# A two-layer hybrid attention transformer on one core: each head pair's keys, queries and values made when its first head is next

## The chip, the cores and the metric

The kernel runs on one core of a Trainium2 chip. The metric is the device time of one execution in microseconds (us). The kernel before took 3505.2 us, the median of 3 runs (3504.65 to 3507.97). The execution that the profiler recorded took 3494.19 us, with a span of 3492.3 us between its first and last recorded instruction.

## The reference, cut to what matters

Two layers work on 1280 tokens (256 of context, 1024 latent), 1024 wide. Each layer modulates its input, projects it, runs three groups of heads side by side (gated linear attention, retention, multi-head latent attention), projects their concatenation, and adds a convolutional feed-forward block. The change touches the latent attention only, called MLA below:

```python
cq  = _rms_norm(p[9],  mla_q_norm_g)                      # 256 wide
q   = _heads(einsum('blr,re->ble', cq, mla_w_uq), 8)
qn, qr = q[..., :64], q[..., 64:]                         # 64 + 32 per head
ckv = _rms_norm(p[10], mla_kv_norm_g)                     # 128 wide
kn  = _heads(einsum('blr,re->ble', ckv, mla_w_uk), 8)     # 64 per head
v   = _heads(einsum('blr,re->ble', ckv, mla_w_uv), 8)     # 64 per head
kr  = p[11]                                               # 32, shared by all heads
...                                                       # axial rotation of qr and kr
s = (einsum('bqhd,bkhd->bhqk', qn, kn) + einsum('bqhr,bkr->bhqk', qr, kr)) * MLA_SCALE
o = einsum('bhqk,bkhe->bqhe', softmax(s), v)
```

Latent queries see all 1280 keys. Context queries see the 256 context keys, and only layer 0 needs them.

## The kernel before

Matrices lie transposed, features on the partitions and the 1280 tokens along the free axis. A float32 product that has to be accurate is made of three products of halves: `split` (L212 on ScalarE, L213 on VectorE) writes the rounded high half and the remainder, and `order` lists high*high, high*low, low*high. Each is one MATMUL with 128 stationary columns and up to 512 moving ones.

A layer goes through input projection, the linear heads (`lin`: states of ten 128-token blocks first, L604 and L612, then the outputs of five groups of 256 tokens), MLA, output projection and feed-forward. `lin` and `mla` are Python generators. A weaver takes about 1.1 steps of one per step of the other, and both start inside the second half of the projection. Program order on each engine is the order in which the weaver runs the steps (a tile framework then sets waits by data and by buffers), so a longer step of `mla` moves everything of `lin` behind it.

MLA has 8 heads, in pairs, since 128 partitions hold two heads of 64. Before head 0, `first` makes, in four steps: the keys of pair 0; the rotated query parts of heads 0 to 3 (`prod_qr(0)`) and the queries of pair 0, and loads head 0; the values of all four pairs (`prod_v`, 30 MATMULs of 512 columns, one for each 128-token block and half product, copied on ScalarE at L874 and stored to the DRAM tensor `vm`); the keys of pairs 1 to 3. `to_memory` stores every key and query chunk of 512 tokens to the DRAM tensor `kq` (L930), and `load` reads a head's 64 rows back (L942, L943) with its rotated part (L944) into the 96-partition buffers `Kt` (two of them, for even and odd heads) and `Q`. During head 0 `rest` runs as side steps, one after each pair of query blocks: load of head 1 and queries of pair 1, queries of pair 2, `prod_qr(1)`, queries of pair 3. The later heads have one side step of DMAs alone (`following`: the next head, and the values of the next pair).

A query block of 128 goes through `scores` (L992, maxima at L994 and L997, exponentials at L1005), `turn` (transposes L1018, copies L1020 and L1022) and `values` (L1042, L1047, L1052). PSUM has eight banks. Scores take two groups of three in turn (`three`), the products take the three banks that the last scores did not (`bank`), and the transposes go into their own scores' banks. The SBUF pools rotate: a tile of `tt` (named t, of 512 columns, split halves and rotation operands among them) has 6 buffers, which `lin` uses too, and such a buffer comes free when the store that reads it has landed. Outputs of a pair gather in one buffer (`ob`, named y) and go to DRAM in two stores a pair (L1056).

The parts that the change touches, with the line numbers of the profile:

Of the kernel before, what the change touches and what calls it, by code (L numbers as in the profile page):

```python
# [74 lines left out]
class Net:  # L75
# [754 lines left out]
    def mla(self, l, S):  # L830
# [14 lines left out]
        V, Q, ob = {}, {}, {}  # L845
# [6 lines left out]
        def weights():  # L852
            t = [self.hid([128, 512], F32R) for _ in range(2)]
            weight("r", a["uqr"][l].rearrange("p k n -> p (k n)"), [[x[:]] for x in t], 1)
            t = self.ws([128, 2, 512], F32R)
            weight("k", a["ukv"][l][:, 0], [[t[:, 0]], [t[:, 1]]], 1)
            t = [self.ws([128, 2, 512], F32R) for _ in range(2)]
            weight("n", a["uqn"][l], [[x[:, 0], x[:, 1]] for x in t], 2)

# [5 lines left out]
        def prod_v():  # L865

            t = [self.hid([128, 512], F32R) for _ in range(2)]
            weight("v", a["ukv"][l][:, 1], [[x[:]] for x in t], 1)
# [7 lines left out]
            W.pop("v")  # L876

        def load_v(p):
            V[p] = [self.hid([128, 5, 128]) for _ in range(2)]
            for i in range(2):  # L880
                nc.sync.dma_start(V[p][i][:], S.vm[:, 5 * i:5 * i + 5, 128 * p:128 * p + 128])
# [5 lines left out]
        def prod_qr(x):  # L887

            terms = [(W["r"][wa][0][:, 256 * kc + 128 * x:256 * kc + 128 * x + 128], S.cq[kc][ca]) for kc in range(2) for wa, ca in order]
# [20 lines left out]
            if x:  # L910
                W.pop("r")

        def prod_k(p):
            hs_ = slice(128 * p, 128 * p + 128)
            to_memory(p, 0, 0, [(W["k"][wa][0][:, hs_], S.ckv[ca]) for wa, ca in order])

        def prod_q(p):
            hs_ = slice(128 * p, 128 * p + 128)
            to_memory(p, 1, lo, [(W["n"][wa][kc][:, hs_], S.cq[kc][ca]) for kc in range(2) for wa, ca in order])

        def to_memory(p, y, o0, terms):

            for o in range(o0, T, 512):
                n = min(512, T - o)
                t = bank()[:, 0:n]
                product(t, o, n, terms)
                hi, lw = self.tt([128, 512], F32R), self.tt([128, 512], F32R)
                self.split(hi[:, 0:n], lw[:, 0:n], t)
                for x, s in enumerate((hi, lw)):
                    nc.sync.dma_start(S.kq[:, p, y, x, o:o + n], s[:, 0:n].bitcast(F32))  # L930
                del hi, lw, s

        def load(h):

            Q[h] = [self.hs([128, T]) for _ in range(2)]
            if h < 2:
                for b in range(2):
                    cs = slice(640 * b, 640 * b + 640)
                    self.split(Kt[h][0][64:96, cs], Kt[h][1][64:96, cs], S.kr[b][64:96, :])
            rows, rot = slice(64 * (h % 2), 64 * (h % 2) + 64), slice(32 * (h % 4), 32 * (h % 4) + 32)  # L940
            for x in range(2):
                nc.sync.dma_start(Kt[h % 2][x][0:64].bitcast(F32), S.kq[rows, h // 2, 0, x])  # L942
                nc.sync.dma_start(Q[h][x][0:64, lo:T].bitcast(F32), S.kq[rows, h // 2, 1, x, lo:T])  # L943
                nc.sync.dma_start(Q[h][x][64:96, lo:T].bitcast(F32), S.qr[rot, h // 4, x, lo:T])  # L944

        def first():
            weights()
            prod_k(0)
            yield
            prod_qr(0)  # L950
            prod_q(0)
            load(0)
            yield
            prod_v()
            yield
            for p in (1, 2, 3):
                prod_k(p)
            load_v(0)
            S.ckv.clear()
            yield  # L960

        def rest():
            load(1)
            S.kr.clear()
            prod_q(1)
            yield
            prod_q(2)
            yield
            prod_qr(1)
            yield  # L970
            prod_q(3)
            S.cq.clear()
            yield

        def following(h):
            load(h)
            if h % 2 == 0:
                load_v(h // 2)
            yield
# [50 lines left out]
        def values(h, qp, pts, sts, nk):  # L1030
# [19 lines left out]
            o = ob[h // 2]  # L1050
            for i in range(2):
                nc.vector.tensor_tensor(o[r:r + 64, 256 * qp + 128 * i:256 * qp + 128 * i + 128],  # L1052
                                        op[64 * i:64 * i + 64, 0], rb[64 * i:64 * i + 64, :], op=ALU.mult)
# [479 lines left out]
```

## Time and profile before

| | |
|---|---|
| median of 3 runs | 3505.2 us (3504.65 to 3507.97) |
| profiled execution | 3494.19 us, span 3492.3 us |
| MLA and linear heads, layer 0 | about 274 to 838 us of the span |
| the same, layer 1 | about 2128 to 2626 us |
| PE (TensorE) busy over the span | 96% |
| VectorE, ScalarE, GpSimd busy | 64%, 44%, 11% |
| weight and other DMA traffic | 410 MB, 117 GB/s on average |

PE is TensorE's matrix unit and PEld its weight loads, DVE is VectorE, ACT ScalarE, POOL GpSimd, and SP the engine that issues the DMAs. Busy PE time is a sum of pipelined durations. What a MATMUL costs in a stream of them is its spacing, which a piece of the chain of waits (the chain that ended last, followed back) gives as a length with a count. A row "ps L885 x6" is six instructions of line 885 that write to PSUM. "kq<-t" is a DMA from SBUF tile t to the DRAM tensor kq. The name `y` in operands of products is the buffer that holds the normalised ckv or cq.

### The profile page before, as it was taken

What the parts mean: (1) busy time and instruction counts of PE and PEld (TensorE: products, weight loads), DVE (VectorE), ACT (ScalarE), POOL (GpSimd) and SP (SyncE); (2) the same over time, 40 slices, a digit from 0 to 9 for tenths busy, and PEclk for the clock granted to TensorE, in tenths of its full rate; (3) what the DMA queues carried; (4) which work ended last, traced back from release to release, by engine and by line L of the source; (5) the groups of instructions that cost most, each with busy time, mean ns of one, the idle gap of its engine ahead of it and who ended that gap; (6) DMA issues with size and microseconds to landing.
All of it is one profiled execution on the core that took longest, in us unless ns stands there. A gap on an engine that the chain in (4) does not pass through costs nothing.

```text
span 3492.3 us, 58230 instructions
## 1 busy us (share of the span) xinstructions
PE 3363.4 (96%) x23310; PEld 2932.7 (84%) x23310; DVE 2225.3 (64%) x3797; ACT 1549.2 (44%) x2881; POOL 399.4 (11%) x627
## 2 busy tenths in 40 slices
PE   8997899999999999999999998899999999999998
PEld 6996677678999999999999997577777888888897
DVE  3434678876774444675557844688877765586555
ACT  3333555554453332343334543555554544345433
POOL 0000244441010000000000000134310010001001
PEclk9998899999999999999999998899999999999999
DMA  7656522234223333432223445532234333223321
GB/s 291 202 176 199 200 77 77 62 92 145 73 73 117 119 121 126 152 103 73 79 73 117 168 135 180 188 84 78 57 101 127 99 94 97 92 95 115 96 92 49
DMA packets 207311, 410.01 MB, mean 117 GB/s; under 512 B 18176, under 2 KB 108096, under 8 KB 207040
## 3 DMA queue, kind: packets, MB, share of 16 engines
q1 hardware_dynamic: 207040, 406.29, 36.8%
q8 instruction: 183, 3.00, 0.4%
q14 instruction: 88, 0.72, 0.1%
HBM read 339.90 MB, written 66.32 MB: 116 GB/s over the span
## 4 chain that ended last, share of the span: by engine, by line
PE 84%; DVE 8%; DMA 3%; ACT 2%; issue 2%; SPq 0%; POOL 0%; DVEq 0%; POOLq 0%; ACTq 0%
PE ps L323 45%; PE ps L1242 16%; PE ps L992 5%; PE ps L1042 3%; PE ps L1018 3%; PE ps L457 3%; PE ps L263 1%; PE ps L647 1%; DVE sm L994 1%; DVE hid L707 1%; PE ps L651 1%; PE ps L885 1%; DMA ws<-in_ada_dram 1%; DVE hid L697 1%; ACT w L1005 1%
## 5 line engine op out<-in xcount | busy, mean ns | idle before, releaser
L323 PE MATMUL ps<-h,w 128*128 128x320 f32 (+5 forms) x9600 | 1664.8, 334 | 12.8 <-ACT h L212 6.3
L323 PEld LDWEIGHTS ps<-h,w 128*128 128x128 f32 x9600 | 1530.6, 189 | 144.2 <-issue 7.1
L213 DVE TENSOR_TENSOR w<-ws,w 128x1024 fp32r<-128x1024 f32 x360 | 441.1, 1226 | 564.7 <-PE ps L323 288.6
L1242 PE MATMUL ps<-hid,w 128*128 128x256 f32 (+4 forms) x3696 | 577.2, 316 | 1.5 <-ACT hid L212 1.4
L1242 PEld LDWEIGHTS ps<-hid,w 128*128 128x128 f32 x3696 | 539.6, 189 | 36.0 <-issue 7.6
L212 ACT CAST w<-ws 128x1024 fp32r<-128x1024 f32 x360 | 379.0, 1054 | 419.5 <-PE ps L1242 291.6
L992 PE MATMUL ps<-h,h 96*128 96x512 f32 (+1 forms) x1200 | 330.3, 395 | 31.6 <-DVE w L1020 11.3
L992 PEld LDWEIGHTS ps<-h,h 96*128 96x128 f32 x1200 | 198.7, 194 | 89.3 <-issue 21.5
L1209 DVE SCALAR_TENSOR_TENSOR t<-u,vec,t 128x642 f32<-128x642 f32 (+3 forms) x176 | 144.6, 822 | 181.6 <-ACT t L1208 181.5
L1203 ACT COPY u<-ps 128x512 f32<-128x512 f32 (+4 forms) x264 | 118.3, 483 | 312.1 <-PE ps L323 312.1
L1005 ACT ACTIVATE w<-ps,sm 128x768 f32<-128x768 f32 (+2 forms) x272 | 208.6, 773 | 101.9 <-DVE sm L1001 78.3
L1247 DVE SCALAR_TENSOR_TENSOR y<-ps,mod,y 128x320 f32<-128x320 f32 (+5 forms) x376 | 197.2, 558 | 68.1 <-PE ps L1242 67.7
L1018 PE MATMUL ps<-ident,w 128*128 128x128 f32 x1312 | 224.7, 287 | 13.1 <-ACT w L1005 12.8
L1038 POOL TENSOR_SCALAR dg<-ident,sm 128x128 f32<-128x128 f32 x144 | 98.9, 690 | 995.0 <-DVE sm L1036 906.4
L1018 PEld LDWEIGHTS ps<-ident,w 128*128 128x128 f32 x1312 | 155.0, 144 | 66.9 <-issue 29.1
L1199 POOL MEMSET u<- 128x1 f32 (+1 forms) x264 | 20.8, 102 | 1613.8 <-DVE t L1210 1436.3
L1042 PE MATMUL ps<-w,hid 128*64 128x128 f32 x2624 | 195.2, 282 | 7.3 <-DVE y L1052 7.1
L994 DVE TENSOR_REDUCE sm<-ps 128x1 f32<-128x1024 f32 x128 | 156.3, 1222 | 58.4 <-PE ps L992 48.4
L1042 PEld LDWEIGHTS ps<-w,hid 128*64 128x64 f32 x2624 | 150.5, 138 | 47.2 <-issue 29.1
L1022 ACT COPY w<-ps 128x256 f32<-128x256 f32 (+1 forms) x272 | 128.0, 473 | 109.4 <-PE ps L1018 106.6
L720 POOL TENSOR_TENSOR hid<-hid,hid 128x512 f32<-128x512 f32 x108 | 147.3, 1381 | 68.1 <-ACT hid L700 48.0
L1208 ACT ACTIVATE t<-u,vec 128x642 f32<-128x642 f32 (+3 forms) x176 | 153.6, 872 | 0.4
(197 smaller groups left out, 3231.8 us busy)
## 6 DMA issues: line engine op xcount, KB each, us to landing
ws<-in_up_dram SPq DMA_DIRECT2D x176, 512.0 KB, 3.6
ws<-in_down_dram SPq DMA_DIRECT2D x88, 512.0 KB, 3.4
ws<-in_ada_dram SPq DMA_DIRECT2D x80, 512.0 KB, 4.9
ws<-in_w_in_dram SPq DMA_DIRECT2D x48, 512.0 KB, 4.3
kq<-t SPq DMA_DIRECT2D x64, 256.0 KB, 2.5
ws<-in_w_out_dram SPq DMA_DIRECT2D x32, 512.0 KB, 3.7
h<-kq SPq DMA_DIRECT2D x48, 320.0 KB, 5.2
y<-in_ada_dram SPq DMA_DIRECT2D x16, 512.0 KB, 8.2
```

Source lines behind the costliest of these rows:

```text
L212: self.nc.scalar.copy(hi, src)
L213: self.nc.vector.tensor_tensor(lo, src, hi.bitcast(F32), op=ALU.subtract)
L323: nc.tensor.matmul(ps[:, i, 0:n], w_[:, k, :], h[k][:, part, o:o + n], start=(k == 0 and q == 0), stop=(k == 7 and q == 2))
L720: nc.gpsimd.tensor_tensor(X[n][:], blk(E[n][:, 0, cs[i]]), qx[:], op=ALU.mult)
L992: nc.tensor.matmul(sc[:, o:o + n], q[qa][0:96, qs], K[ka][0:96, o:o + n], start=(x == 0), stop=(x == 2))
L994: nc.vector.tensor_reduce(st[:, 1:2], sc[:, 0:1024], axis=AX.X, op=ALU.max)
L1005: nc.scalar.activation(P[:, c0:c1], sc[:, c0:c1], AF.Exp, bias=st[:, 2:3], scale=MSCALE, accum_out=st[:, 3 + j:4 + j])
L1018: nc.tensor.transpose(ps[:, t_], P[:, 128 * (t0 + t_):128 * (t0 + t_) + 128], self.ident[:])
L1042: nc.tensor.matmul(op[64 * i:64 * i + 64, 0], V[h // 2][t_ // 5][:, t_ % 5, r:r + 64], pts[i][:, t_], start=(t_ == 0), stop=(t_ == nk - 1) ...
L1208: nc.scalar.activation(v[:, 0:n], u[:, 1:1 + n], AF.Identity, scale=cw(j, 1), bias=self.vec[l][:, V_CB + j:V_CB + j + 1])
L1242: nc.tensor.matmul(pb[i][:, 0:n], w[w_][:, x, ms], p.hh[f0 + x][hp][:, o - 1:o - 1 + n], start=(x == 0 and q == 0), stop=(x == gn - 1 and ...
L1247: nc.vector.scalar_tensor_tensor(t, pb[i][:, o:o + n], self.md(l, 5, m, who), t, op0=ALU.mult, op1=ALU.add)
```

## The change

Nothing is left of `first`, `rest`, `following`, `prod_v` over all pairs, `vm` and `ob`. For each pair there are three steps: keys, queries, values. Those of pair 0 run before head 0 (after `prod_qr(0)`), those of pair p during the odd head 2p-1, one step after each pair of query blocks, with `prod_qr(1)` ahead of them in head 3. An even head has a side step of DMAs alone, `load`, for the odd head after it. A key or query chunk now goes by two DMAs per half: rows 0 to 63 straight to the even head's buffer, rows 64 to 127 to `kq` (64 partitions now), from which `load` reads them. The values of a pair are 30 MATMULs of 128 columns into three PSUM banks, and two ScalarE copies of 640 columns put them into the buffers that `values` reads. The weights for values and rotated queries are loaded and split 128 columns at a time (`some`). The output of each head and pair of query blocks goes to a small tile of 256 columns and from there to DRAM, 64 rows of 1 KB per store.

```diff
-        V, Q, ob = {}, {}, {}
+        V, Q = {}, {}
...
+        def some(src, n):
+            raw, t = self.tt([128, n, 128]), self.hid([128, 2, n, 128], F32R)
+            nc.sync.dma_start(raw[:], src)
+            self.split(t[:, 0], t[:, 1], raw[:])
+            return t
...
+        def prod_v(p):
+            w = some(a["ukv"][l][:, 1:2, 128 * p:128 * p + 128], 1)
+            V[p] = [self.hid([128, 5, 128]) for _ in range(2)]
+            b = flip[0] ^ 3
+            ps = self.ps[:, b:b + 3, :].rearrange("p a b -> p (a b)")
             for t_ in range(10):
-                p = bank()
                 for x, (wa, ca) in enumerate(order):
-                    nc.tensor.matmul(p, S.ckv[ca][:, 128 * t_:128 * t_ + 128], W["v"][wa][0], start=(x == 0), stop=(x == 2))
-                s = self.tt([128, 512])
-                nc.scalar.copy(s[:], p)
-                nc.sync.dma_start(S.vm[:, t_, :], s[:])
...
+                    nc.tensor.matmul(ps[:, 128 * t_:128 * t_ + 128], S.ckv[ca][:, 128 * t_:128 * t_ + 128], w[:, wa, 0],
+                                     start=(x == 0), stop=(x == 2))
             for i in range(2):
-                nc.sync.dma_start(V[p][i][:], S.vm[:, 5 * i:5 * i + 5, 128 * p:128 * p + 128])
+                nc.scalar.copy(V[p][i][:].rearrange("p a b -> p (a b)"), ps[:, 640 * i:640 * i + 640])
+            yield
...
+        def prod_kq(p):
+            h = 2 * p
+            Q[h] = [self.hs([128, T]) for _ in range(2)]
...
+            turned(h)
             hs_ = slice(128 * p, 128 * p + 128)
...
+            for y in range(2):
...
+                for o in range(lo if y else 0, T, 512):
+                    n = min(512, T - o)
+                    t = bank()[:, 0:n]
+                    product(t, o, n, terms)
+                    parts = [self.tt([128, 512], F32R) for _ in range(2)]
+                    self.split(parts[0][:, 0:n], parts[1][:, 0:n], t)
+                    for x, s in enumerate(parts):
+                        nc.sync.dma_start((Q[h] if y else Kt[0])[x][0:64, o:o + n].bitcast(F32), s[0:64, 0:n].bitcast(F32))
+                        nc.sync.dma_start(S.kq[:, p, y, x, o:o + n], s[64:128, 0:n].bitcast(F32))
+                    del parts, s
+                yield
...
+        def load(p):
+            h = 2 * p + 1
             Q[h] = [self.hs([128, T]) for _ in range(2)]
...
+            turned(h)
             for x in range(2):
...
+                nc.sync.dma_start(Kt[1][x][0:64].bitcast(F32), S.kq[:, p, 0, x])
+                nc.sync.dma_start(Q[h][x][0:64, lo:T].bitcast(F32), S.kq[:, p, 1, x, lo:T])
             yield
...
-            o = ob[h // 2]
+            o = self.tt([128, 256])
...
-            if h % 2 and qp in (2, 4):
-                c0, c1 = (lo, 768) if qp == 2 else (768, T)
-                nc.sync.dma_start(S.m[:, 4 + h // 2, c0:c1], o[:, c0:c1])
-
-        for _ in first():
+            nc.sync.dma_start(S.m[r:r + 64, 4 + h // 2, 256 * qp:256 * qp + 256], o[r:r + 64])
+
+        def chain(*gs):
+            for g in gs:
+                yield from g
+
+        weights()
+        for _ in chain(prod_qr(0), prod_kq(0), prod_v(0)):
             yield
...
-            side = rest() if h == 0 else following(h + 1) if h < 7 else iter(())
+            side = chain()
+            if h % 2 == 0:
+                side = load(h // 2)
+            elif h < 7:
+                p = (h + 1) // 2
+                side = chain(*[prod_qr(1)] * (p == 2), prod_kq(p), prod_v(p))
```

On PE, at the start of layer 0's head 0, the kernel before has this order. L604 and L612 are the states of `lin`'s blocks, L872 the values, L885 the key products, L992 head 0's first scores.

```order
L604 MATMUL ps<-ident,hid_3137 128x128 x4
L612 MATMUL ps<-hid_3135,hid_3152 32x64 x12
L872 MATMUL ps<-hid_3154,y_374 128x512
L872 MATMUL ps<-hid_3154,y_375 128x512
...
L612 MATMUL ps<-hid_3135,hid_3152 32x64 x4
L885 MATMUL ps<-y_374,ws_2576 128x512
L885 MATMUL ps<-y_375,ws_2576 128x512
...
L992 MATMUL ps<-h_2566,h_2774 128x256
```

In the changed kernel the same place reads as follows; L877 are the values of pair 0, and L968 the scores.

```order
L604 MATMUL ps<-ident,hid_3105 128x128 x4
L612 MATMUL ps<-hid_3103,hid_3120 32x64 x16
L877 MATMUL ps<-hid_3185,y_373 128x128
L877 MATMUL ps<-hid_3185,y_374 128x128
...
L968 MATMUL ps<-h_2565,h_2709 128x256
...
L994 MATMUL ps<-ident,w_3253 128x128
L604 MATMUL ps<-ident,hid_3227 128x128 x4
```

The 30 wide value products became 30 narrow ones, and the 27 key products of pairs 1 to 3 are gone from between them and the first scores.

In head 1 of layer 0, PE now has side steps. This is the end of pair 1's query products (L885), the scores behind them, and further down the values of pair 1 (L877) with the scores behind those. L994 are the transposes, L1018 the weighted sums of values, L1023 the spread of the denominators.

```order
L885 MATMUL ps<-y_378,ws_2574 128x256
L885 MATMUL ps<-y_377,ws_2575 128x256
L968 MATMUL ps<-h_2567,h_3355 128x512
...
L1023 MATMUL ps<-dg_4259,ones 64x128
L1018 MATMUL ps<-w_4229,hid_3189 64x128
L877 MATMUL ps<-hid_4181,y_373 128x128
L877 MATMUL ps<-hid_4181,y_374 128x128
...
L968 MATMUL ps<-h_2567,h_3355 128x512
L968 MATMUL ps<-h_2567,h_3356 128x512
```

Before, such rows stand in head 0 only; behind each of them come the next scores, whose three banks are the ones that the products have just filled.

On SP, the queue that issues the DMAs, two chunks of pair 1's queries before (L930), with what follows them:

```order
L930 DMA kq_372<-t_3474 128x512
L930 DMA kq_372<-t_3475 128x512
L930 DMA kq_372<-t_3486 128x512
L588 DMA hid_3397<-gqk_89 128x256
L590 DMA hid_3399<-v_88 128x2x256
```

And the end of the same queries now (L942 to the even head's buffer h, L943 to kq), with the head outputs (L1030), the value weights (L861) and loads of `lin` behind them:

```order
L942 DMA h_3968<-t_4109 64x256
L943 DMA kq_372<-t_4109 64x256
L942 DMA h_3969<-t_4110 64x256
L943 DMA kq_372<-t_4110 64x256
L659 DMA hid_4157<-gate_86 128x2x256
L1030 DMA m_87<-t_4167 64x256
L861 DMA t_4180<-in_ukv_dram 128x128
L683 DMA u_4486<-gB_91 128x2x256
L1030 DMA m_87<-t_4329 64x256
L676 DMA m_87<-hid_4021 128x2x256
```

A chunk's halves take four issues instead of two, and each pair of query blocks adds an output store to the queue.

## Rows read from the trace of the kernel before

**Rows 1.** Page, busy time by engine and the chain that ended last.
```profile
PE 3363.4 (96%) x23310; PEld 2932.7 (84%) x23310; DVE 2225.3 (64%) x3797; ACT 1549.2 (44%) x2881; POOL 399.4 (11%) x627
PE 84%; DVE 8%; DMA 3%; ACT 2%; issue 2%; SPq 0%; POOL 0%; DVEq 0%; POOLq 0%; ACTq 0%
```
**Rows 2.** Stretches: length, busy time by engine, granted clock, DMA share, GB/s.
```profile
465.00:838.00 373.00, 351.48 (x3089) 264.73 (x3088) 300.21 (x658) 206.33 (x534) 143.23 (x148) 0.97 0.29 83
2300.00:2577.00 277.00, 264.35 (x2320) 199.80 (x2320) 229.35 (x474) 149.19 (x378) 100.34 (x106) 0.98 0.27 74
290.00:346.00 56.00, 37.50 (x367) 30.80 (x366) 26.36 (x50) 22.19 (x66) 0.00 (x0) 0.72 0.82 233
346.00:366.00 20.00, 16.84 (x85) 12.45 (x75) 6.88 (x14) 11.21 (x24) 0.00 (x0) 0.93 0.79 296
366.00:465.00 99.00, 89.76 (x758) 68.19 (x757) 73.06 (x173) 51.19 (x140) 32.80 (x33) 0.90 0.47 143
2216.00:2300.00 84.00, 78.37 (x702) 59.90 (x703) 67.90 (x153) 45.59 (x122) 29.73 (x29) 0.96 0.50 153
```
**Rows 3.** Chain, layer 0's start of heads: start us, us, what.
```profile
346.24 8.41 PE ps L872 x30
...
358.14 2.49 DMA kq<-t
...
361.44 2.65 DMA kq<-t
...
364.93 0.64 PE ps L992 x3
...
375.66 0.44 PE ps L604 x4
```
**Rows 4.** Chain, layer 1's start of heads.
```profile
2195.95 6.49 PE ps L872 x21
...
2203.12 4.25 DMA vm<-t
...
2215.89 0.97 PE ps L992 x3
...
2225.81 0.73 PE ps L604 x4
```
**Rows 5.** Chain, six key or query products, full clock.
```profile
2228.68 1.40 PE ps L885 x6
```
**Rows 6.** Timeline, 128 float32 weight columns with four moving columns.
```profile
440.56 0.50 PE L739 MATMUL ps<-hm,hid 128*128 128x4 f32 x4
```
**Rows 7.** Tile t, 275 to 465 us: splits, copies, stores; ns min/median/max.
```profile
L930 SPq DMA_DIRECT2D kq<-t x48: 319/399/1816, 282.2 to 416.7; - x48
L212 ACT CAST t<-ps x24: 372/585/637, 281.6 to 413.2; 128x512 fp32r<-128x512 f32 x16, 128x256 fp32r<-128x256 f32 x8
L213 DVE TENSOR_TENSOR t<-ps,t x24: 413/681/692, 282.3 to 415.7; 128x512 fp32r<-128x512 f32 x16, 128x256 fp32r<-128x256 f32 x8
...
  DMA kq<-t: 5.4, 6
```
**Rows 8.** Chain by line, 465 to 838 us, cut by the view.
```profile
by line: PE ps L992 18.1%; PE ps L1042 13.3%; PE ps L1018 11.7%; PE ps L647 5.5%; DVE sm L994 4.7%; DVE hid L707 4.1%; issue 4.0%; PE ps L651 3.7%; DVE hid L697 3.0%; PE ps L731 2.7%; PE ps L670 2.3%; DVE w L1020 2.2%; PE ps L814 2.1%; ACT 
```
**Rows 9.** DMA issues, 275 to 420 us: count, KB each, median us to landing.
```profile
kq<-t SPq DMA_DIRECT2D x32, 256.0 KB, 2.5
...
h<-kq SPq DMA_DIRECT2D x8, 320.0 KB, 6.6
...
v<-t SPq DMA_DIRECT2D x3, 128.0 KB, 2.6
```
**Rows 10.** Waits, 465 to 838 us: us in total, times, longest us.
```profile
DVE sm L994 <- PE ps L992: 23.8, 21, 3.0
...
PE ps L1018 <- ACT w L1005: 6.3, 6, 2.1
...
PE ps L992 <- DVE w L1020: 4.0, 3, 3.0
```

More of the change, by code (lines that the diff above doesn't have):

```diff
@@ L852, in weights @@
         def weights():
-            t = [self.hid([128, 512], F32R) for _ in range(2)]
-            weight("r", a["uqr"][l].rearrange("p k n -> p (k n)"), [[x[:]] for x in t], 1)
             t = self.ws([128, 2, 512], F32R)
@@ L887, in prod_qr @@
         def prod_qr(x):
-            terms = [(W["r"][wa][0][:, 256 * kc + 128 * x:256 * kc + 128 * x + 128], S.cq[kc][ca]) for kc in range(2) for wa, ca in order]
+            w = some(a["uqr"][l][:, :, 128 * x:128 * x + 128], 2)
+            terms = [(w[:, wa, kc], S.cq[kc][ca]) for kc in range(2) for wa, ca in order]
             for o in range(lo, T, 512):
@@ L909, in prod_qr @@
                 del hi, raw, s, r
-            if x:
-                W.pop("r")
-        def prod_k(p):
-            hs_ = slice(128 * p, 128 * p + 128)
[L915 to L931, printed above, removed]
@@ L933, in load @@
-        def load(h):
-            Q[h] = [self.hs([128, T]) for _ in range(2)]
[L936 to L940, printed above, removed]
-            for x in range(2):
-                nc.sync.dma_start(Kt[h % 2][x][0:64].bitcast(F32), S.kq[rows, h // 2, 0, x])
-                nc.sync.dma_start(Q[h][x][0:64, lo:T].bitcast(F32), S.kq[rows, h // 2, 1, x, lo:T])
-                nc.sync.dma_start(Q[h][x][64:96, lo:T].bitcast(F32), S.qr[rot, h // 4, x, lo:T])
@@ L946, in first @@
[L946 to L978, printed above, removed]
+            del w, terms
+            yield
+        def turned(h):
+            for x in range(2):
+                nc.sync.dma_start(Q[h][x][64:96, lo:T].bitcast(F32), S.qr[32 * (h % 4):32 * (h % 4) + 32, h // 4, x, lo:T])
+        def prod_kq(p):
+            h = 2 * p
+            Q[h] = [self.hs([128, T]) for _ in range(2)]
+            if p == 0:
+                for K in Kt:
+                    for b in range(2):
+                        cs = slice(640 * b, 640 * b + 640)
+                        self.split(K[0][64:96, cs], K[1][64:96, cs], S.kr[b][64:96, :])
+                S.kr.clear()
+            turned(h)
+            hs_ = slice(128 * p, 128 * p + 128)
+            for y in range(2):
+                if y:
+                    terms = [(W["n"][wa][kc][:, hs_], S.cq[kc][ca]) for kc in range(2) for wa, ca in order]
+                else:
+                    terms = [(W["k"][wa][0][:, hs_], S.ckv[ca]) for wa, ca in order]
+                for o in range(lo if y else 0, T, 512):
[8 more added lines that the diff above has]
+                    del parts, s
+                yield
@@ L1049, in values @@
             nc.scalar.copy(rb[:], op[:, 1])
-            o = ob[h // 2]
+            o = self.tt([128, 256])
             for i in range(2):
-                nc.vector.tensor_tensor(o[r:r + 64, 256 * qp + 128 * i:256 * qp + 128 * i + 128],
+                nc.vector.tensor_tensor(o[r:r + 64, 128 * i:128 * i + 128],
                                         op[64 * i:64 * i + 64, 0], rb[64 * i:64 * i + 64, :], op=ALU.mult)
-            if h % 2 and qp in (2, 4):
-                c0, c1 = (lo, 768) if qp == 2 else (768, T)
-                nc.sync.dma_start(S.m[:, 4 + h // 2, c0:c1], o[:, c0:c1])
-        for _ in first():
+            nc.sync.dma_start(S.m[r:r + 64, 4 + h // 2, 256 * qp:256 * qp + 256], o[r:r + 64])
[4 more added lines that the diff above has]
+        for _ in chain(prod_qr(0), prod_kq(0), prod_v(0)):
             yield
@@ L1348 @@
         S.qr = net.dp.tile([128, 2, 2, T], F32, name=f"qr{l}")
-        S.kq = net.dp.tile([128, 4, 2, 2, T], F32, name=f"kq{l}")
-        S.vm = net.dp.tile([128, 10, 512], F32, name=f"vm{l}")
+        S.kq = net.dp.tile([64, 4, 2, 2, T], F32, name=f"kq{l}")
         S.ckv = [net.yk(F32R) for _ in range(2)]
```

7 lines of the change are left out of this document (removed).

## The prediction, made before the changed kernel ran

> **What bounds the kernel now.** I read the page first: busy time by engine, then the chain that ended last. The reader is to see that PE is busy for 96% of the span and carries 84% of the chain, with VectorE at 8% and DMA at 3% [rows 1]. A change that adds PE time therefore costs nearly all of it, unless it takes away one of the few places where PE waits. Next I read the stretches that the change touches, by engine. Layer 0's heads behind the start keep PE busy for 351.48 of 373.00 us, 0.94, and layer 1's for 264.35 of 277.00 [rows 2]; DMA is at 0.29 and 0.27 there, so the DMA engines have room. The start is another matter: from 290 to 346 us DMA is at 0.82, PE is busy for 37.50 of 56 us and its granted clock is 0.72, between its two levels of 1.2 and 2.4 GHz; from 346 to 366 us DMA is at 0.79 [rows 2]. The chain through that place says what ends last: all values in one run of 8.41 us, then key chunks that wait for their stores, 2.49 and 2.65 us, before head 0's first scores at 364.93 [rows 3]. In layer 1 it is the same with a 4.25 us wait for a store of the values, and first scores at 2215.89 [rows 4]. So there are about 20 us in each layer in which the heads could begin and don't. The waits of the heads and the DMA issues came last, for what the side steps would run into [rows 7, 9, 10].
>
> **The start of the heads.** The change takes two things from between `lin`'s states and the first scores: the wide values, and the keys of pairs 1 to 3 with their stores. In their place come 30 MATMULs of 128 columns, for pair 0. Prices: six products of 512 columns take 1.40 us, 0.233 each [rows 5]. For a narrow product the weights decide: four MATMULs with only four moving columns take 0.50 us [rows 6], and four of 128 columns take 0.44, 0.11 each, at the better clock [rows 3] and 0.73, 0.18 each, at the poorer [rows 4]. The values of pair 0 are then 3.3 to 5.4 us; I take the middle, 4.4. The values of before began at 346.24 and 2195.95, when all that they need was there, so the scores should begin at 350.6 and 2200.4 in place of 364.93 and 2215.89: **-14.3 us and -15.5 us**. Here the split tiles no longer hold up PE, since only pair 0 is made.
>
> The Trainium skill has another price for the narrow products: "TensorE: Matmul & The Clock Gate", section "Back-to-back issue gap", states some 81 ns sustained for 128 columns with a weight load each, and by it the four rows of 0.11 would be 0.08. Those rows are float32 and these products are not, so no row settles it.
>
> **DMA at the start.** Head 0's keys and queries are no longer read back: four loads of 320 KB, half of the eight that the view of the start lists for heads 0 and 1 [rows 9], 1.3 MB. At 233 GB/s [rows 2] that is 5.6 us of transfer a layer in a stretch where DMA is at 0.82 but PE and VectorE work too. It is worth between nothing and 5.6; I take half, **-2.8 us a layer**. The products of pair 0 stay ahead of head 0 and change places among themselves, which I cost at nothing: the states of `lin` run beside them.
>
> **The work that comes into the later heads.** The queries of pairs 1 to 3 and `prod_qr(1)` move from head 0 to the odd heads at the same price, from a stretch with granted clock 0.90 to one with 0.97 [rows 2]; that may be worth a microsecond, which I leave in the range. New there are the keys of pairs 1 to 3, three half products of 512, 512 and 256 columns each, 3 x 2.5 x 0.233 = 1.75 us, 5.25 for three pairs; and the values of three pairs, 90 narrow products of 0.11, 9.9 us. Together PE gets 15.15 us a layer. How much reaches the end lies between the PE lines that the chain names, 59.4% when the eight are added [rows 8], and the busy share, 0.94: 9.0 to 14.2 us. I take 0.65, since the row is cut with 22.6% of the chain not named: 9.8 us. The keys bring VectorE three splits a pair, 2 x 0.68 + 0.41, 5.3 us in all [rows 7], of which I let a quarter reach the end, the named VectorE lines of the chain being 14% [rows 8]: 1.3. In all **+11.2 us a layer**, the same in both, since keys and values always cover 1280 tokens. ScalarE's two copies a pair replace ten of 512 columns for all pairs, and it is busy for 206 of 373 us [rows 2]; I cost them at nothing.
>
> **Stalls behind the side steps.** This is the unknown. A side step fills the three banks that the next scores want, and VectorE must split each chunk before they are free. With six tile buffers, two of which `lin` may hold, the third chunk of a step waits for the stores of the first to land. Before, 24 chunks waited 5.4 us so [rows 7], 0.23 a chunk, 0.7 a step. Now each chunk has two more issues on SP at 0.40 us [rows 7], so I take 0.7 + 0.8 = 1.5 us a step; behind the waiting split on VectorE stand the maxima of the next scores, and PE waits for those. Six key and query steps a layer make 9.0, less the 2.1 of the three query steps of before, 6.9, and half of that can lie beside transposes and `lin`: **+3.5 us a layer**. The bounds are 0 and 17.7 (the second rival). A value step takes no such tiles but for its small weight load; its last copy stands between it and the scores, one ScalarE copy of 0.59 us [rows 7] or so, and is covered by the scores of the first bank.
>
> The output tiles cost nothing by the sum. Each is a store of 128 KB of which nothing waits but its buffer; such stores land in 2.6 us [rows 9], and there is one for each pair of query blocks. "Perfetto Trace Analysis", section "DMA Optimizations", in the Trainium skill speaks against them: transfers under 2 KB carry an overhead each and should be batched, and here the rows are 1 KB where they were 2 KB and more. At a DMA share of 0.29 the trace gives that rule nothing to act on in the heads [rows 2], and the sum would be the same by it.
>
> **The sum.** Layer 0: -14.3 - 2.8 + 11.2 + 3.5 = -2.4. Layer 1: -15.5 - 2.8 + 11.2 + 3.5 = -3.6. Together -6.0 us. All durations are from the profiled execution of 3494.19 us, which is 11 us under the median of the runs, 3505.2; the difference of 6.0 is carried over to the median: **3499.2 us**, 0.17% less, just within the 0.2% (7 us) that a measurement of this kernel can tell from no change. It is the small rest of two terms of about 30 us of opposite sign: what is taken from before head 0 is mostly given back inside the odd heads.
>
> **The rivals.** (1) The narrow products are not held by their weights and cost a quarter of the wide ones, 0.058 us. For it: the rows at 0.11 are of float32 operands; against it: four moving columns cost no less than 128 [rows 3, 6]. Then pair 0 costs 1.6 us less and the other pairs 90 x 0.052 x 0.65 = 3.0 less, a layer: -9.2, **3490 us**. By the Trainium skill's 81 ns it would be about half of that, 3494.
>
> (2) The side steps in the odd heads stall PE for a whole store: split tiles come free only when both stores of a half have landed, 2.5 us [rows 9] and 0.8 us of issues, in each of the six key and query steps: 19.8 less 2.1 = 17.7 us a layer in place of 3.5. Result **3527.6 us**. The kernel is slower than before as soon as more than 6.5 us a layer of such stalls reach the end. For it: output tiles now take buffers of the same pool; against it: in the heads PE waited at its scores for only 4.0 us and at its transposes for 6.3 [rows 10], in a stretch without side steps of products.
>
> (3) The heads begin earlier but gain only half: head 0 runs into `lin`'s remaining state blocks and their loads, which were ready in time only because the values and keys took so long. That gives back 14.9 us, **3514 us**. For it: DMA is as full ahead of that place as in it [rows 2]; against it: those loads stood in the queue behind the very stores that go.
>
> **How the numbers follow.** Chances: forecast 0.42 (its own range 3490 to 3508; it counts 0.20 as faster, 0.20 as same, 0.02 as slower), rival 1 0.20 (0.17, 0.03, 0), rival 2 0.22 (0, 0.02, 0.20), rival 3 0.16 (0.03, 0.06, 0.07). So faster 0.40, same 0.31, slower 0.29. The low end is rival 1 with the full relief of DMA (-5.6) and no stalls (-7.0), 3478; the high end is near rival 2, 3526.
>
> **What would show it.** The first scores of layer 0 about 14 us nearer to the end of `lin`'s eighth state block, with 30 narrow products alone between them. The narrow products at 0.11 us each in the heads; at 0.06 rival 1 holds. In the odd heads, idle time of PE at the scores behind a side step of 1 to 2 us; 3 us and more, with the split tiles' stores as releasers, is rival 2. PE idle in head 0 for DMAs of `lin` is rival 3. The prediction is wrong if the heads' stretch grows by other work than those 15 us, or if the start does not shorten.

## The result: 36 us slower, and the profile after

The changed kernel took 3540.8 us (median of 4 runs, 3539.2 to 3548.5) beside 3504.9 us for the kernel before on the same chip (3503.4 to 3508.0): a ratio of 1.0106, 95% interval 1.0088 to 1.0123. The forecast was 3499.2 us with a range up to 3526. It had the wrong sign, and the result lies outside its range.

Three slips of the texts above have to be named first, since they matter below. A side step follows each block of 128 queries, not each pair of blocks: there are eight slots in a head in layer 0 and six in layer 1, and the three or four steps of an odd head fall into successive slots, one block apart. An output store is 64 KB, 64 rows of 1 KB, not 128 KB. And the scores behind the values are not head 0's first. Part of head 0's scores run ahead of the values in both kernels, though `mla` issues the values ahead of all scores, so PE's order is not simply the order of the generators. In layer 0, the kernel before and then the changed one:

```profile
318.98 0.28 PE L992 MATMUL ps<-h,h 96*128 96x256 f32 x1
321.52 0.66 PE L992 MATMUL ps<-h,h 96*128 96x256 f32 x2 [2.26 <-DMA h<-qr]
```

```profile
319.66 1.22 PE L968 MATMUL ps<-h,h 96*128 96x256 f32 x3 [0.97 <-DMA h<-t]
323.95 2.08 PE L968 MATMUL ps<-h,h 96*128 96x256 f32 x6
```

In layer 1 it is nine scores in both, from 2164.44 and 2204.74 us on. What the forecast calls the first scores are the next ones that the chain names behind the values.

First the page of the changed kernel, the lines that answer to [rows 1]:

```profile
PE 3397.9 (96%) x23490; PEld 2969.6 (84%) x23490; DVE 2218.1 (63%) x3805; ACT 1548.5 (44%) x2885; POOL 398.6 (11%) x627
PE 86%; DVE 7%; ACT 3%; issue 2%; DMA 2%; SPq 0%; POOL 0%; DVEq 0%; POOLq 0%; ACTq 0%
```

The reader is to see that PE is busy for 34.5 us longer, three quarters of the loss between the two profiled executions (3494.2 and 3539.2 us, 45.0 apart; the medians differ by 35.9). VectorE's busy time did not grow. PE has 180 MATMULs more; the rest of its growth needs another reason.

The chain through the start of the heads in layer 0, for [rows 3] (start us, us, what):

```profile
341.72 1.08 PE ps L612 x32
342.80 6.59 PE ps L877 x30
349.39 0.75 PE ps L968 x3
...
355.40 0.85 PE ps L604 x4
```

and in layer 1, for [rows 4]:

```profile
2226.27 6.59 PE ps L877 x30
2232.86 2.68 PE ps L968 x6
```

The next scores do begin right behind the narrow values, with no split and no store between. From the start of the values to these scores are 6.6 us in both layers, against 18.7 and 19.9 before: 12.1 and 13.3 us won, of 14.3 and 15.5 forecast. The narrow values ran at 0.22 us each here, at the lower of the two clock levels, a granted clock of 0.50:

```profile
342.80:349.40 6.60, 6.60 (x31) 6.60 (x32) 0.57 (x2) 1.25 (x5) 0.00 (x0) 0.50 0.38 127
```

So the time is lost behind this place. The values of pair 2 show the price that was forecast:

```profile
585.67 3.04 PE ps L968 x9
588.72 2.64 PE ps L877 x24
```

2.64 us for 24 are 0.11 each. Those of pair 1, at 439.66 us, took 5.10 us for 30, 0.17 each.

Now the stretches (length, busy time of PE, PEld, DVE, ACT, POOL, granted clock, DMA share, GB/s), for [rows 2]: the lead, the start with head 0, heads 1, 3 and 5, all heads but the first in layer 0, and in layer 1.

```profile
290.00:343.00 53.00, 35.60 (x375) 28.75 (x374) 25.85 (x49) 21.00 (x66) 0.00 (x0) 0.74 0.84 228
343.00:398.00 55.00, 51.38 (x432) 39.21 (x432) 38.33 (x90) 30.09 (x89) 18.68 (x18) 0.82 0.10 29
398.00:473.00 75.00, 68.72 (x543) 52.94 (x541) 49.10 (x113) 33.72 (x84) 18.00 (x21) 0.93 0.30 76
526.00:611.00 85.00, 72.00 (x527) 54.12 (x525) 58.75 (x115) 39.65 (x103) 21.79 (x22) 0.90 0.33 93
665.00:739.00 74.00, 66.30 (x545) 50.18 (x543) 48.43 (x113) 34.97 (x92) 28.50 (x28) 0.91 0.46 138
398.00:863.00 465.00, 427.99 (x3575) 325.52 (x3573) 342.80 (x758) 238.01 (x607) 157.04 (x164) 0.94 0.32 90
2277.00:2671.00 394.00, 372.62 (x3212) 288.49 (x3210) 296.99 (x640) 210.96 (x521) 120.55 (x130) 0.97 0.32 88
```

The same stretches in the kernel before, heads 1, 3 and 5, then all heads but the first in layer 0 and in layer 1:

```profile
436.00:490.00 54.00, 53.73 (x468) 40.12 (x467) 38.49 (x99) 27.73 (x70) 15.70 (x18) 1.00 0.32 86
546.00:603.00 57.00, 53.46 (x444) 40.03 (x443) 47.38 (x93) 31.97 (x87) 22.15 (x22) 0.94 0.24 65
658.00:717.00 59.00, 53.22 (x493) 40.49 (x490) 49.02 (x109) 30.66 (x83) 28.48 (x28) 0.94 0.27 70
436.00:838.00 402.00, 380.39 (x3362) 287.09 (x3361) 319.49 (x717) 220.91 (x572) 154.55 (x161) 0.97 0.30 84
2276.00:2626.00 350.00, 336.58 (x3005) 258.90 (x3004) 284.76 (x608) 195.69 (x490) 118.06 (x128) 0.99 0.28 80
```

The odd heads take 75, 85 and 74 us in layer 0; the same heads took 54, 57 and 59 before (from the first scores of a head to those of the next). By the forecast's prices their new work is 8.6 us of PE each (1.75 for keys, 3.5 for queries, 3.3 for values), and some 6 more in head 3 for `prod_qr(1)`. The granted clock is 0.93, 0.90 and 0.91 in them, and it was 1.00, 0.94 and 0.94. Over heads 1 to 7 PE's busy time grew by 47.6 us in layer 0 and 36.0 in layer 1, and its idle time by 15.4 and 8.0. The work that came in is some 32 and 28 us by the forecast's prices, an estimate, so part of the growth of busy time is the lower clock. DMA around head 0 fell from 0.79 and 0.47 to 0.10, as meant, but the lead ahead of the values still has it at 0.84, with a clock of 0.74.

What PE waited for in the same stretch of layer 0 (us in total, times, longest), for [rows 10]:

```profile
PE ps L994 <- ACT w L981: 13.0, 11, 2.4
PE ps L968 <- DVE t L213: 6.1, 4, 2.3
PE ps L968 <- DVE t L902: 5.2, 2, 4.0
PE ps L1018 <- DVE t L1028: 4.8, 5, 2.3
```

Transposes wait for exponentials (13.0 us; 6.3 before, by the same view from 436 to 838 us as well as in [rows 10]), and scores wait for the split or the rotation of a side step that holds their banks (11.3 us; before, this stretch had no such step). And of the waits for the stores of split tiles, from the view of tile t in this stretch:

```profile
  DMA kq<-t: 3.1, 2
```

3.1 us in two waits, one of ScalarE and one of VectorE; in layer 1's heads the view has no such line. The second rival named these stores as the cause of the stalls. They are too small for it.

### The profile page after: what moved, and what is told of

It reads as the page before. It is cut to its first block, busy times and chain, and to the rows that moved or that the text cites. A ratio compares the mean times of both kernels' runs of the same rounds, so it can differ in the third digit from the quotient of the medians.

```text
span 3537.0 us, 58752 instructions
## 1 busy us (share of the span) xinstructions
PE 3397.9 (96%) x23490; PEld 2969.6 (84%) x23490; DVE 2218.1 (63%) x3805; ACT 1548.5 (44%) x2885; POOL 398.6 (11%) x627
## 4 chain that ended last, share of the span: by engine, by line
PE 86%; DVE 7%; ACT 3%; issue 2%; DMA 2%; SPq 0%; POOL 0%; DVEq 0%; POOLq 0%; ACTq 0%
PE ps L323 45%; PE ps L1224 15%; PE ps L968 5%; PE ps L1018 4%; PE ps L994 3%; PE ps L457 3%; PE ps L263 1%; DVE sm L970 1%; PE ps L647 1%; PE ps L885 1%; PE ps L877 1%; ACT w L981 1%; PE ps L651 1%; DVE hid L707 1%; PE ps L354 1%
## 5 line engine op out<-in xcount | busy, mean ns | idle before, releaser
L323 PE MATMUL ps<-h,w 128*128 128x320 f32 (+5 forms) x9600 | 1665.4, 334 | 14.3 <-ACT h L212 6.3
L968 PE MATMUL ps<-h,h 96*128 96x512 f32 (+1 forms) x1200 | 338.9, 404 | 25.9 <-DVE t L213 10.1
L968 PEld LDWEIGHTS ps<-h,h 96*128 96x128 f32 x1200 | 207.6, 202 | 83.4 <-issue 20.2
L994 PE MATMUL ps<-ident,w 128*128 128x128 f32 x1312 | 227.5, 291 | 20.7 <-ACT w L981 20.5
L994 PEld LDWEIGHTS ps<-ident,w 128*128 128x128 f32 x1312 | 155.8, 146 | 76.8 <-ACT w L981 33.0
L1018 PE MATMUL ps<-w,hid 128*64 128x128 f32 x2624 | 203.7, 285 | 10.3 <-DVE t L1028 8.0
L1018 PEld LDWEIGHTS ps<-w,hid 128*64 128x64 f32 x2624 | 154.4, 140 | 51.7 <-issue 35.3
```

Source lines behind the costliest of these rows:

```text
L323: nc.tensor.matmul(ps[:, i, 0:n], w_[:, k, :], h[k][:, part, o:o + n], start=(k == 0 and q == 0), stop=(k == 7 and q == 2))
L968: nc.tensor.matmul(sc[:, o:o + n], q[qa][0:96, qs], K[ka][0:96, o:o + n], start=(x == 0), stop=(x == 2))
L994: nc.tensor.transpose(ps[:, t_], P[:, 128 * (t0 + t_):128 * (t0 + t_) + 128], self.ident[:])
L1018: nc.tensor.matmul(op[64 * i:64 * i + 64, 0], V[h // 2][t_ // 5][:, t_ % 5, r:r + 64], pts[i][:, t_], start=(t_ == 0), stop=(t_ == nk - 1) ...
```

## The experiments

Two theories went in. **A**: the loss is the clock. The dense products ahead of head 0 are gone, so the heads start at the poorer level and dip again. **B**: the loss is in the side steps of the odd heads. A whole key or query product with its three splits fills the banks of the next scores and VectorE's queue, in heads where VectorE is at 0.8 already [rows 2]. Each run is given with its ratio to the kernel before, run on the same chip. Kernels that ran on different chips are to be compared by these ratios. Their intervals reach 3 to 7 us to either side, so a difference of 5 us or less between two such kernels is not clear of noise. A stretch of a single trace also moves by some us from one execution to the next.

**One part of the change at a time.** The small outputs alone, in the kernel before:

```diff
-            o = ob[h // 2]
+            o = self.tt([128, 256])
...
+            nc.sync.dma_start(S.m[r:r + 64, 4 + h // 2, 256 * qp:256 * qp + 256], o[r:r + 64])
```

> The kernel before with one part of the change: the small output tiles and their stores. Theory A (the clock: the start of the heads and the odd heads run longer at the poorer level since the dense products are gone) and theory B (side steps in the odd heads stall PE and load VectorE where it is already at 0.8) both expect no change, within 0.2% of before (3498 to 3512 us). A third, that the small stores and their buffers cost the time, expects +10 us or more.

Measured: 3503.0 us, ratio 0.9998 (0.9986 to 1.0010). The output part costs nothing, as forecast.

The values alone, in the kernel before (narrow products, those of pairs 1 to 3 in odd heads; keys and queries as they were):

```diff
-            prod_v()
-            yield
+            yield from prod_v(0)
...
-            load_v(0)
-            S.ckv.clear()
             yield
...
             load(h)
-            if h % 2 == 0:
-                load_v(h // 2)
             yield
+            if h % 2 == 0:
+                yield from prod_v(h // 2)
```

> The kernel before with one part of the change: values per pair by narrow products, those of pairs 1 to 3 in the odd heads; keys and queries as before. Warm narrow products cost 0.11 us: 90 in the heads are 9.9 us a layer, 30 ahead of head 0 take 3.3 to 6.4 in place of 8.2. By the price alone: +5 to +8 us a layer, 3515 to 3521. Theory A adds little, since the dense key products still stand ahead of head 0: about the same, 3515 to 3525. Theory B adds nothing, value steps need no split: 3515 to 3521.

Measured: 3515.6 us, ratio 1.0033 (1.0023 to 1.0044): 12 us, the price by 0.11 us a product. Both theories expected it.

The other way round, the changed kernel with the wide values of before put back ahead of head 0 (`prod_v` and `load_v` as before; the odd heads take `vs(p)` in place of `prod_v(p)`):

```diff
-        for _ in chain(prod_qr(0), prod_kq(0), prod_v(0)):
+        def vs(p):
+            if p == 0:
+                prod_v()
+            load_v(p)
+            yield
+        for _ in chain(prod_qr(0), prod_kq(0), vs(0)):
```

> The changed kernel with the values of all pairs made ahead of head 0 again by 30 wide products and stored to DRAM; keys, queries and outputs as changed. By the price alone 6.3 us a layer less than changed, 3528. Theory A: the wide products also bring the clock up before head 0, a further 5 to 8 us a layer, 3512 to 3518. Theory B: the stalls in the odd heads remain, 3525 to 3530.

Measured: 3511.3 us, ratio 1.0024 (1.0014 to 1.0033). Keys, queries and outputs as changed cost 8 us, the values 12, but both together 36: some 16 us (with an uncertainty of 8, by the intervals) belong to neither alone. It came out a little under what A said, but where it came from does not speak for A. Heads 1 and 5 of layer 0 became 13.3 and 8.7 us shorter, heads 0 and 2 4.2 and 5.0 us longer: in the odd heads the value step costs far more than 3.3 us when it is the third whole step in a row.

**The clock at the start.** Thirty wide products without a use, put ahead of the values of pair 0 in the changed kernel:

```diff
             b = flip[0] ^ 3
+            if p == 0:
+                for x in range(30):
+                    nc.tensor.matmul(self.ps[:, b + x % 3, :], S.ckv[0][:, 128 * (x % 10):128 * (x % 10) + 128], W["k"][0][0], start=True, stop=True)
```

> The changed kernel with 30 wide products without a use put ahead of the values of pair 0 (their results are overwritten). They cost 7.0 us a layer at the better clock and up to 14 at the poorer. Theory A: they bring the clock up for head 0, which gives back what they cost or more: 3530 to 3545. Theory B: the full price, 3555 to 3568.

Measured: 3534.9 us, ratio 1.0089 (1.0069 to 1.0109), 6 us less than changed, with 60 MATMULs more. The intervals of the two overlap, so all that is shown is that the products cost nothing. That is inside A's figures, but the trace takes most of A's meaning away. In layer 0 the products ran from 314.2 to 327.4 us, between the states of `lin`, where PE waited in the changed kernel. The lead had a better clock, 0.87 where it was 0.74:

```profile
290.00:341.00 51.00, 39.99 (x399) 31.49 (x401) 25.85 (x49) 21.10 (x64) 0.00 (x0) 0.87 0.79 221
```

The values of pair 0 began 1.5 us earlier than changed, still at 0.22 us each; and head 0 behind them, from the end of these values to head 1's first scores, is the same (this kernel, then the changed one):

```profile
347.80:396.60 48.80, 45.13 (x405) 33.06 (x404) 37.97 (x88) 29.13 (x85) 18.87 (x19) 0.86 0.06 18
```

```profile
349.40:398.20 48.80, 45.18 (x403) 33.01 (x404) 37.96 (x88) 29.13 (x85) 18.88 (x18) 0.86 0.06 17
```

Same length, same clock of 0.86. So the useless products raised the clock of the lead, not that of head 0. What a warm head 0 would be worth was not reached by this edit, and stays open.

**Finer side steps.** In the changed kernel, for pairs 1 to 3 a step is one chunk of 512 tokens. Same instructions, but an odd head of layer 0 has seven side steps in place of three (eight in place of four in head 3), one of layer 1 six (seven in head 3):

```diff
                     del parts, s
-                yield
+                    if p:
+                        yield
+                if not p:
+                    yield
```

> The changed kernel with the key and query products of pairs 1 to 3 cut into side steps of one chunk of 512 tokens each, so that seven slots of an odd head are used in place of three. Theory B (the steps hold the banks of the next scores and queue their splits on VectorE): the idle time of PE behind them falls, 5 to 12 us, 3528 to 3535. Theory A (the clock alone): no change, 3538 to 3543; where PE idles less in the odd heads the clock may dip less as well.

Measured: 3510.3 us, ratio 1.0020 (1.0010 to 1.0029): 30 us less than changed, far more than B had expected, by an edit that adds and removes no work. Heads 1 and 5 of layer 0, all heads but the first in layer 0, and in layer 1 now read

```profile
399.00:468.00 69.00, 65.68 (x553) 49.61 (x552) 52.26 (x118) 34.61 (x89) 19.17 (x22) 1.00 0.33 85
...
653.00:720.00 67.00, 63.58 (x569) 48.56 (x568) 52.73 (x116) 35.29 (x93) 28.81 (x28) 0.97 0.48 135
399.00:839.00 440.00, 414.39 (x3565) 311.97 (x3565) 342.28 (x756) 236.99 (x607) 154.78 (x164) 0.98 0.34 94
2255.00:2644.00 389.00, 376.16 (x3212) 286.95 (x3210) 295.62 (x640) 210.06 (x521) 119.95 (x130) 0.98 0.32 89
```

and PE's waits in layer 0

```profile
PE ps L997 <- ACT w L984: 8.7, 10, 2.1
PE ps L971 <- DVE t L902: 5.2, 2, 4.0
PE ps L971 <- DVE t L213: 4.9, 6, 2.3
```

Against the changed kernel's 465 us the stretch of layer 0 is 25 us shorter: PE's idle time fell from 37.0 to 25.6 us, and its busy time from 428.0 to 414.4 with nearly the same MATMULs, as the granted clock rose from 0.94 to 0.98. In layer 1 only 5 us came back (394 to 389 us). So in layer 0 whole steps cost twice, once as waits, and once by a lower clock; that it is the waits which lower the clock fits these rows, but no run tests it apart. The start, with its clock, was left as changed. The size of the steps in the odd heads is thereby shown as the larger part of the loss, as B says, with A's clock as a part of B's price. Which of the things that a step holds up (the banks, VectorE's queue, the late exponentials) costs most is not shown: the waits for exponentials fell from 13.0 to 8.7 us, those for splits from 6.1 to 4.9, and those for the rotation, which was not cut up, stayed at 5.2.

> The same finer steps in the kernel with wide values ahead of head 0 (3511.3 us). Theory B: 3500 to 3506, and so it may be as fast as before. Theory A: 3509 to 3513.

The same edit in the kernel with wide values: 3488.9 us, ratio 0.9966 (0.9953 to 0.9979), 22 us less than with whole steps (20 by the ratios) and 14 less than before. Beyond B's figure again.

**What added PE work costs in an odd head.** Products of pairs 1 to 3 run twice over (the first result is overwritten), with whole steps and with finer ones:

```diff
-                    product(t, o, n, terms)
+                    for _ in range(2 if p else 1):
+                        product(t, o, n, terms)
```

> The kernel with wide values (3511.3 us) with each key and query product of pairs 1 to 3 run twice over (the first result is overwritten): 15.75 us of PE work more in layer 0's odd heads and 13.65 in layer 1's, at the better clock, and no more splits. Prediction's share of 0.65: +19 us, 3530. If all PE work there reaches the end: +29, 3541. If the dense work lifts the clock in these heads (theory A) it is less than the share says, 3520 to 3530.

> The kernel with wide values and finer steps (3488.9 us) with each key and query product of pairs 1 to 3 run twice over: 29.4 us of PE work more at the better clock, in the odd heads. Where the steps were whole products, the same work cost 4 us (3511.3 to 3515.6) while the time at the poorer clock fell by 35 us. If spread steps leave PE bound by its work, 20 to 30 us more: 3509 to 3519. If the added work is again paid by the clock or lies in waits: 3489 to 3498.

Measured: 3515.6 us with whole steps, ratio 1.0040 (1.0025 to 1.0055), 4 us for 29 us of work (6 by the ratios) and less than any of the three figures expected; 3511.7 with finer ones, ratio 1.0026 (1.0016 to 1.0037), 23 us for the same work (21 by the ratios), as expected of spread steps. Behind a whole step in layer 0 PE was not the bound, and more products found room there; where the steps are spread, 0.7 to 0.8 of the work reaches the end. The stretch behind head 0 in layer 0, whole steps, once and twice:

```profile
402.00:843.60 441.60, 408.57 (x3469) 304.64 (x3466) 340.35 (x753) 232.26 (x597) 155.28 (x162) 0.97 0.34 97
```

```profile
402.00:843.00 441.00, 414.97 (x3528) 315.14 (x3528) 338.35 (x750) 232.39 (x596) 154.83 (x162) 0.98 0.34 97
```

6.4 us more of PE in the same 441 us, for 15.75 us of added work: idle time filled, and a clock of 0.98 in place of 0.97. In layer 1 the same stretch grew from 375 to 381 us. What the bound was instead in layer 0 shows in the chain of the changed kernel's head 3, behind the rotation (L901 to L904) and its splits:

```profile
549.39 0.69 PE ps L968 x3
...
553.91 0.69 DVE hid L336
554.60 0.60 DVE t L902
555.20 0.60 DVE hid L338
555.80 0.15 DVE hid L904
...
556.32 0.42 DVE sm L973
556.73 0.60 DVE hid L339
557.33 0.07 DVE hid L213
...
559.14 0.34 DVE hid L903
559.47 0.33 DVE t L902
```

For these microseconds the chain is VectorE's queue: the step's rotation and split between the operations of a norm of `lin` (L336 to L339) and the maxima of the scores (L973).

**Other places for the steps.** The kernel before with only the keys of pairs 1 to 3 moved, into side steps of head 0:

```diff
-            for p in (1, 2, 3):
-                prod_k(p)
             load_v(0)
-            S.ckv.clear()
             yield
...
             prod_q(1)
             yield
+            prod_k(1)
+            yield
...
+            prod_k(3)
+            S.ckv.clear()
+            yield
```

> The kernel before with only the keys of pairs 1 to 3 moved, from ahead of head 0 into side steps of head 0. Takes 27 dense products and their waits for stores (9 us in layer 0, 13 in layer 1) from the start. Theory A: head 0 stands behind the wide values still and starts warm, so little is lost: 3498 to 3504. Theory B: VectorE is less loaded in head 0 than in the odd heads, so the steps cost about their price there: 3500 to 3506. A loss of more than 5 us would say that neither is enough.

Measured: 3489.9 us, ratio 0.9968 (0.9954 to 0.9982): 13 us less than before (11 by the ratio), and less than either theory expected. In its trace the next scores follow the start of the values after 9.1 and 9.5 us, where it was 17.4 and 18.7 by the same view, and head 0 behind them is 7.3 and 5.4 us longer for 5.25 us of keys. Head 0 of layer 0, behind the values:

```profile
356.10:435.70 79.60, 70.04 (x564) 52.43 (x557) 59.25 (x128) 41.85 (x117) 24.36 (x24) 0.91 0.58 192
```

These are whole steps too, seven of them, and here they cost little beyond their work. VectorE is busy for 0.74 of this stretch with the steps in it, while heads 1, 3 and 5 of the kernel before have it at 0.71, 0.83 and 0.83 without any. So it may be the room on VectorE that makes the difference, but no run changes that load alone. The traced execution was the slowest of five (3498.0 us), so its trace shows only a part of the 13 us.

The rotated queries of heads 4 to 7 in head 2 in place of head 3, a chunk to a step, with wide and with narrow values (both with finer steps):

```diff
                 del hi, raw, s, r
+                if x:
+                    yield
             del w, terms
-            yield
+            if not x:
+                yield
...
-                side = load(h // 2)
+                side = chain(load(h // 2), *[prod_qr(1)] * (h == 2))
...
-                side = chain(*[prod_qr(1)] * (p == 2), prod_kq(p), vs(p))
+                side = chain(prod_kq(p), vs(p))
```

> The kernel with wide values and finer key and query steps (3488.9 us), with the rotated queries of heads 4 to 7 made in head 2 in place of head 3, one chunk to a side step. Head 3 is the longest left in that trace (77 us in layer 0 beside 60 in heads 1 and 5, with 13.7 us at the poorer clock and 5.6 us of scores waiting for the rotation). Theory B, with the clock falling after each stall: 8 to 16 us less in all, 3473 to 3481. If it is the work alone, which only moves, no change: 3486 to 3491.

> The same edit in the changed kernel with finer steps (3510.3 us); values by narrow products per pair as changed. Theory B: 8 to 16 us less, 3494 to 3502, and then the changed kernel with nothing but its side steps spread is not slower than before, while the price of narrow values (12 us) and the cold start are still in it. The work alone: 3507 to 3512.

Measured: 3486.6 us, ratio 0.9951 (0.9938 to 0.9965), and 3511.8, ratio 1.0016 (1.0007 to 1.0025). By the ratios that is 5 us and 1 us less than without, and neither is clear of noise. B's 8 to 16 us did not come. In the first, head 3 of layer 0 fell from 77 to 61 us and head 2 rose from 55 to 69; the 7.1 us of scores waiting for the rotation went, and transposes waited 11.1 us for exponentials where it had been 7.2. Not every wait behind a side step is to be had back. The kernel with wide values, finer steps and this edit has the lowest time of the study, 0.5% under the kernel before.

> The changed kernel with finer steps (3510.3 us) and 30 wide products without a use ahead of the values of pair 0, which cost 14 us or more by their price. With whole steps the same edit made 6 us less. Theory A, a cold start as a loss of its own beside the steps: again 3 to 10 us less, 3500 to 3508. If the steps were all of it and the 6 us came from the odd heads: 14 us more, 3522 to 3530.

The useless products in the changed kernel with finer steps: 3502.8 us, ratio 0.9998 (0.9988 to 1.0008), 8 us less than without them, and here the intervals do not overlap. The traces have both leads shorter: the values of pair 0 begin 3.4 us earlier in layer 0, and 7.4 us earlier in layer 1 from the end of layer 0's heads; with whole steps it was 1.5 and 4.6. So it looks like a gain in the lead, independent of the odd heads. But layer 1's lead differs by 5 us between other traces as well (that of the small outputs alone beside that of the kernel before, whose times are equal), so where the 8 us lie is not shown for certain.

## Why the prediction was wrong

**The step that failed is the term "stalls behind the side steps".** It stood at 3.5 us a layer, 7 in all. Spreading the same steps gave back 30 us, 25 of them in layer 0's heads and 5 in layer 1's, and that is the least that they cost. The reasoning behind the 3.5 names the banks of the next scores and the maxima behind the splits, but it prices only the wait for stores, by [rows 7]. Those waits are 3.1 us. It has no price for VectorE's queue in heads where `lin` already keeps it at 0.8 [rows 2], for the exponentials and transposes that come late behind it, and for the clock, which fell to between 0.90 and 0.93 in the odd heads of layer 0 and whose part in the 25 us is 13.6. The queries and `prod_qr(1)` were moved "at the same price" from head 0 and expected to gain by a better clock; they were moved into heads where VectorE is busier, three or four whole steps in a row with the values, and the clock there fell.

**The share of PE work that reaches the end, 0.65,** came from a stretch without product steps. It is 0.78 with spread steps and 0.14 with whole ones, by the doubled products (0.72 and 0.19 by the ratios). One share for both cannot be right, and the small figure is no good news: it says that something else holds the head.

**The values** were sized right at the better clock, and too low in the sum. Narrow products at the better clock take 0.11 us, 2.64 us for 24, so the first rival, 0.058, is out. That their weights hold them is the forecast's reading of [rows 6] and fits, but no run tests it. The Trainium skill states some 0.081 us for 128 columns ("TensorE: Matmul & The Clock Gate", section "Back-to-back issue gap"). This trace does not agree: it shows 0.11. By the forecast's terms the values were worth 5 us in all (4.4 - 8.4 at the start, 9.9 x 0.65 in the heads, two layers); alone they measured 12. Those of pair 0 took 6.6 us, not 4.4, at the poorer clock.

**The start** was right as a mechanism, 12.1 and 13.3 us between the values and the next scores, though these are not the first scores of the head. That a part of it can be kept is shown by the keys moved into head 0. **The DMA relief** of 2.8 us a layer is not shown: the values of pair 0 began 3.4 us earlier in layer 0, but 5 us later in layer 1, counted from the end of layer 0's heads. The kernel with the small outputs alone has the same 5 us there at the time of the kernel before, so this may be the spread of single traces.

**The outputs** cost nothing, as said, though the size of a store was given wrong. The rule on small DMAs in the Trainium skill ("Perfetto Trace Analysis", section "DMA Optimizations") had no effect in this case: the small outputs alone gave a ratio of 0.9998.

**The rivals.** The second came nearest in time (3527.6) and in place, the side steps of odd heads, and had the wrong mechanism. The third, a head 0 that runs into `lin`'s states, is not seen: head 0 behind the values takes 48.8 us in layer 0 with PE busy for 45.2, and none of PE's waits there is for a DMA. What its lower clock of 0.86 costs is the part that stays open.

**The sum as measured:** -6 forecast; +23 for the stalls (30 in place of 7); +7 for the values (12 in place of 5); +4.4 for the start (25.4 won in place of 29.8); +5.6 for the DMA relief that did not come. That is +34, beside the 36 measured. The terms are from different experiments and not independent. The 4.4 us are the values of pair 0 at the lower clock, which took 6.6 us in the run with the values alone too and so stand in the 12 as well, and the last term rests on two leads of single traces. The agreement is rough, and in part luck.

## What to carry to other kernels

When work is moved beside other work, ask first which engine behind it has a queue there, and how many pieces it comes in: the same products in six to eight pieces a head cost 30 us less than in three or four, while whole pieces in head 0 cost little beyond their work. A share of hidden work read from a stretch without such pieces does not price them. And waits of a busy matrix engine can be charged twice, since the clock may be lower beside them, here 0.94 in place of 0.98.

## What was not expected of the hardware

Nearly the same MATMULs took 428.0 us of busy PE in whole steps and 414.4 us in spread ones, with a granted clock of 0.94 and 0.98. And work without a use made a kernel faster: 60 MATMULs ahead of the heads took 8 us off the kernel with finer steps; with whole steps it was 6 us, which is not clear of noise.
